# One recurrence step of a chunked delta rule with two head pairs on opposite quarters of the array

## The chip, the cores and the metric

The kernel runs on one core of one Trainium2 chip. The metric is the time of one execution in device microseconds. Engines: PE is TensorE, DVE is VectorE, ACT is ScalarE, POOL is GpSimd, SP is SyncE, which issues the DMAs.

## What is computed

One decoder layer on 512 tokens of width 1024: a combined projection, dilated attention, RWKV-7 time mixing, two branch gates, an output projection and a gated feed-forward network with a short convolution. Everything is float32; the large products are made of three products of rounded float32 halves (hi x hi, hi x lo, lo x hi), each with 512 moving columns. The part that the change touches is the recurrence of the time mixing, over 16 heads of 64 channels:

```python
def step(state, inp):
    r_t, w_t, k_t, v_t, aa_t, bb_t = inp
    sa = jnp.einsum('bhvk,bhk->bhv', state, aa_t)
    state = state * w_t[:, :, None, :] + sa[..., None] * bb_t[:, :, None, :] + v_t[..., None] * k_t[:, :, None, :]
    return state, jnp.einsum('bhvk,bhk->bhv', state, r_t)

_, y = lax.scan(step, state0, (tm(r_h), tm(w_h), tm(k_h), tm(v_h), tm(-kk), tm(kk * a_h)))
mean = jnp.mean(y, axis=-1, keepdims=True)
var = jnp.mean(jnp.square(y - mean), axis=-1, keepdims=True)
y = ((y - mean) * lax.rsqrt(var + GN_EPS)).reshape(b, s, c) * lnx_w + lnx_b
```

## The kernel before

**Groups, pairs, chunks.** The 512 tokens are cut into 8 chunks of 64 (`NCH`, `C`). The 16 heads make 8 pairs of 128 channels, two pairs make a group, and the four groups are worked through in turn. For a pair, `pair()` makes the projections k, r and v (24 products each), the decays, the tile `ar` (in each chunk 64 columns of a-rows and 64 of r-rows), the tile `bk` and the products of both, the gram tile `gt`, masked on DVE (`mask`, L1396). `inverse(g)` (L1429) then inverts the triangular blocks of a group: a long row of small DVE instructions, two batches of 32x32 products on PE (`pe`), and copies on DVE and ACT. `chain(g)` (L1565) runs the recurrence of the group's two pairs, chunk by chunk.

**One chunk of a chain**, in the order in which it must happen: `state` (L1610) adds the products of the state `mbd` with `ar` (two of 128 rows by 128 columns of the array) and of the values with `gt` (four of 64 by 64) in a PSUM tile `xy`. Half of its partitions, `X`, is the right side of the solve, the other half, `R`, the start of the chunk's output; which is which changes with the parity of the chunk, because a pair's tiles hold even and odd chunks with their halves swapped. `xs` (L1619) copies the half `X`, 64 partitions by 256 columns (two pairs side by side), to SBUF on ACT; `solve` (L1629) multiplies it with the inverse (four of 64 by 64); an ACT copy (L1658) brings the result, again 64 by 256, into the other half of the tile `uv`; `update` (L1633) makes the state's addition `w` from it (four of 128 by 64, which alternate between the two column halves), `carry` (L1638) scales and adds on DVE into `mbd`, with `mp` from POOL. Off this path `outs` (L1645) adds the last part of the output in `xy[R]`, and `out` (L1649) copies it into `yts`. Every second chunk `values` (L1584) centres the next two chunks' values and two ACT copies (`value`) put them into `uv`. After the chain `norm` scales `yts`, `turn` (L1710) transposes it, and `y` and `gated` (L1719, L1723) finish each pair on DVE. A float32 product is recorded as two MATMUL rows.

**What sets the order.** `Plan` (L47) simulates the engines with a cost in microseconds for each task and writes the instructions in the order in which its engines would take them. A chain's steps have priority 0 and go first; the 512-column products fill PE in between: while chains 0 to 2 run, the projections of the groups to come (k, r, v) and 16 branch gates (`pg` with 512 columns); while chain 3 runs, the attention's output projection (`pa`). A pair of group 2 can start only when chain 0 has given its buffers back, one of group 3 when chain 1 has, and a chain needs its group's inverse. After chain 3 `rwkv_out` and everything behind it run in the order of the code. The order is fixed when the kernel is built: on the chip every engine takes its own instructions strictly in that order and waits where data is late.

Of the kernel before, what the change touches and what calls it, by code (L numbers as in the profile page):

```python
# [18 lines left out]
P = 128  # L19
# [109 lines left out]
class Layer:  # L129
# [278 lines left out]
    def begin(self):  # L408
        self.rw_ctx = ExitStack()
        one = ("col wv v12 o1 row qk00 qk10 qk01 qk11 qk02 qk12 t kk2 fb fk ein cs bk rk km sh l2 l2l gp0 gp1 inv xs mp g2 "  # L410
               "sq yts").split()
        two = "raw w mm sp acc ht wvraw v0 attT sc sm pr pts pt po araw2 acc2 px xy k gg y ld psb".split()
        self.pl = Plan(**{x: 1 for x in one}, **{x: 2 for x in two}, uv=3, araw=10, ekraw=4)
# [809 lines left out]
    def pair(self, g, i):  # L1223
# [20 lines left out]
        def halves(t, x):  # L1244

            f = t.rearrange("p (t e) n -> p t (e n)", e=2)
# [75 lines left out]
        def a_row():  # L1322
            d["ar"] = gp.tile([P, NCH, P], F32, tag="ar", name=self.n("ar"), bufs=2)

            d["bkt"] = [gp.tile([P, 4, P], F32, tag="bkt", name=self.n("bkt")) for q in range(2)]
            nc.vector.scalar_tensor_tensor(halves(d["ar"], 1), c8(d["k"]), ch(self.kkn), pex(), op0=ALU.mult,
                                           op1=ALU.mult)
# [5 lines left out]
        ar = dve(0.75, a_row, [k, ex, gr["room"]])  # L1333
# [6 lines left out]
        def norm():  # L1340

            pn = d["pn"] = self.psx("pn")
            for t in range(4):
                self.mm(pn[:, 2 * t : 2 * t + 2], d["kk2"][:, t * P : (t + 1) * P], self.sel2, t == 0, t == 3)

        def norms():
            if i == 0:
                gr["sq"] = gp.tile([P, 16], F32, tag="sq", name=self.n("sq"), bufs=1)
            for x in range(2):
                nc.scalar.copy(gr["sq"][64 - 64 * x : 128 - 64 * x, 8 * i : 8 * i + 8], d["pn"][64 * x : 64 * x + 64, :8])  # L1350
# [33 lines left out]
        def gram(q):  # L1384
# [4 lines left out]
            for cc in range(4):  # L1389
                col = (cc % 2) * 2 + cc // 2  # L1390
# [174 lines left out]
    def chain(self, g):  # L1565
# [18 lines left out]
        def values(c):  # L1584
            for i in range(2):
                self.mm(d["u"][:, i * P : (i + 1) * P], prs[i]["v"][:, c * C : (c + 2) * C], self.cen, i == 0, i == 1)

        def value(c, x):
            uv = uvs[c + x] = cw.tile([P, 256], F32, tag="uv", name=self.n("uv"), bufs=3)
            nc.scalar.copy(uv[64 * x : 64 * x + 64, :], d["u"][64 * x : 64 * x + 64, :])  # L1590
# [5 lines left out]
        norms, all_ = [], []  # L1596

        def vals(c):
            t = pe(0.54, lambda: values(c), [start, last_uv])
            for x in range(2):  # L1600
                uvd[c + x] = sca(0.38, lambda x=x: value(c, x), [t], C_ + 0.01 * x, take=("uv",))
        vals(0)
        for c in range(NCH):
            e, q, cp = c % 2, c // 4, (c % 4) // 2
            r0, x0 = (0, 64) if e == 0 else (64, 0)
            R, X = slice(r0, r0 + 64), slice(x0, x0 + 64)
            gt = lambda i, h, rows, cols, e=e, q=q, cp=cp: prs[i]["gt"][rows, e, 4 * q + 2 * cp + h, cols]
# [11 lines left out]
            def xs(s=s, X=X):  # L1619
                s["xs"] = cw.tile([P, 256], F32, tag="xs", name=self.n("xs"), bufs=1)  # L1620
                nc.scalar.copy(s["xs"][X, :], s["xy"][X, :256])
# [23 lines left out]
            def outs(c=c, s=s, gt=gt, R=R):  # L1645
                for j, (i, h, cs) in enumerate(hs):
                    self.mm(s["xy"][R, cs], gt(i, h, slice(0, P), R), s["uv"][:, cs], c == 0 and j == 0, j == 3)

            def out(c=c, s=s, R=R):  # L1649
                if c % 2 == 0:  # L1650
                    yts[c // 2] = cw.tile([P, 256], F32, tag=f"yt{c // 2}", name=self.n("yt"), bufs=1)
                nc.scalar.copy(yts[c // 2][R, :], s["xy"][R, :256])

            st = pe(1.1 if c else 0.56, state, [uvd[c], start] + mb, take=("xy",), name=f"xy{g}.{c}")
            x = sca(0.38, xs, [st], take=("xs",))
            mpt = pl.add("POOL", 1.06, mp, mb, C_, take=("mp",)) if 0 < c < NCH - 1 else None
            so = pe(0.56, solve, [x, last_uv], give=("xs",), name="u")
            last_uv = sca(0.38, lambda s=s, X=X: nc.scalar.copy(s["uv"][X, :], d["u"][X, :]), [so])  # L1658
            prev = mb
            if c < NCH - 1:  # L1660
                up = pe(0.5, update, [last_uv], name="w")
                mb = [dve(0.36, lambda i=i, carry=carry: carry(i), [up, mpt], give=("mp",) if mpt and i else ())
# [3 lines left out]
            ou = pe(0.47, outs, [last_uv], C_ + 0.02, name="xr")  # L1666
            yt = sca(0.38, out, [ou], C_ + 0.05, take=("yts",) if c == 0 else (), give=("xy",))
            pl.join([ou] + ([up] if c < NCH - 1 else []), give=("uv",))
# [7 lines left out]
        fin = []  # L1676
        for i in range(2):
# [32 lines left out]
            def turn(i=i):  # L1710
                ys["p", i] = py = ps("t")
                for t in range(4):
                    self.tr(py[:, t * P : (t + 1) * P], yts[t][:, i * P : (i + 1) * P], t == 0, t == 3)

# [3 lines left out]

            def y(i=i, m=m):  # L1719
                nc.vector.scalar_tensor_tensor(ys[i], ys["p", i], self.col["lnx_w"][:, m : m + 1], ys[i],  # L1720
                                               op0=ALU.mult, op1=ALU.add)
# [10 lines left out]
            yl = pl.add("DMA", 0.8, y_load, [d["yt", 5], prs[i]["bvs"]], M_, take=("y",), lag=2.0)  # L1732
            tu = pe(0.95, turn, norms, min(S_, T_), take=("t",), name="ty")
            fin.append(tu)
            t = dve(0.75, y, [tu, yl], E_, give=("t",))
            t = dve(0.75, gated, [t, gt_], T_, give=("gg",))
# [10 lines left out]
    def norm(self, yts, t, deps, T_):  # L1747
# [3 lines left out]
        y4 = lambda: yts[t].rearrange("p (h e) -> p h e", e=64)  # L1751
# [386 lines left out]
```

## Time and profile before

| what | value |
|---|---|
| three runs | 1253.78, 1249.96, 1244.15 us; median 1249.96 |
| profiled execution, its own time | 1247.44 us |
| its span, first to last instruction | 1245.7 us |
| PE busy | 1197.4 us (96%) |
| DVE, ACT, POOL busy | 746.5, 545.4, 118.2 us |
| chain 0, first product to last | 441.7 to 493.0 us of the span |
| chain 3, first product to last | 714.9 to 766.8 us of the span |

In the timeline a row is a run of like instructions; the difference between the starts of two rows that follow each other on PE is what the first took of PE's time, since products overlap at their ends. A name such as `128*64` says which part of the array a product holds: 128 rows (the depth of the sum) by 64 columns (output partitions).

### The profile page before, as it was taken

What the parts mean: (1) busy time and instruction counts of PE and PEld (TensorE: products, weight loads), DVE (VectorE), ACT (ScalarE), POOL (GpSimd) and SP (SyncE); (2) the same over time, 40 slices, a digit from 0 to 9 for tenths busy, and PEclk for the clock granted to TensorE, in tenths of its full rate; (3) what the DMA queues carried; (4) which work ended last, traced back from release to release, by engine and by line L of the source; (5) the groups of instructions that cost most, each with busy time, mean ns of one, the idle gap of its engine ahead of it and who ended that gap; (6) DMA issues with size and microseconds to landing.
All of it is one profiled execution on the core that took longest, in us unless ns stands there. A gap on an engine that the chain in (4) does not pass through costs nothing.

```text
span 1245.7 us, 18047 instructions
## 1 busy us (share of the span) xinstructions
PE 1197.4 (96%) x7012; PEld 976.5 (78%) x7012; DVE 746.5 (60%) x1242; ACT 545.4 (44%) x981; POOL 118.2 (9%) x235
## 2 busy tenths in 40 slices
PE   4999999999999999999999799999999999999997
PEld 3788878888787877777787577788888888878886
DVE  6697862422678968536896844555556566552235
ACT  4484522523566373455445343334443434442133
POOL 4000000000001013030002222214100000000001
PEclk9899999999999999999999789999999999999999
DMA  9745871130333332322330424571133332323331
GB/s 316 242 143 163 274 235 49 46 85 1 92 99 88 97 89 77 110 60 82 92 105 26 146 79 132 174 219 34 56 97 96 90 102 85 102 87 116 102 119 68
DMA packets 168900, 139.39 MB, mean 112 GB/s; under 512 B 8849, under 2 KB 150251, under 8 KB 168815
## 3 DMA queue, kind: packets, MB, share of 16 engines
q1 hardware_dynamic: 168671, 137.98, 36.5%
q8 instruction: 55, 0.90, 0.3%
q14 instruction: 30, 0.25, 0.1%
q10 hardware_dynamic: 144, 0.26, 0.1%
HBM read 127.65 MB, written 10.56 MB: 111 GB/s over the span
## 4 chain that ended last, share of the span: by engine, by line
PE 82%; DVE 8%; DMA 5%; ACT 2%; issue 1%; SPq 0%; POOL 0%; POOLq 0%; DVEq 0%; ACTq 0%
PE u L148 23%; PE o L148 13%; PE v L148 7%; PE pg L148 7%; PE qk L148 6%; PE xy L148 4%; PE pr L148 3%; DMA araw<-in_w_ada_dram 3%; PE k L148 3%; PE pa L148 2%; PE r L148 2%; PE early L148 2%; PE po L148 2%; PE sc L148 1%; PE pt L151 1%
## 5 line engine op out<-in xcount | busy, mean ns | idle before, releaser
L194 DVE TENSOR_TENSOR wlo<-raw,whi 128x1024 fp32r<-128x1024 f32 x67 | 84.1, 1255 | 151.0 <-ACT whi L193 150.9
L148 PE MATMUL u<-h2lo,whi 128*128 128x512 f32 (+2 forms) x368 | 142.3, 387 | 0.0
L148 PE MATMUL u<-h2hi,whi 128*128 128x512 f32 (+2 forms) x368 | 142.3, 387 | 0.0
L148 PE MATMUL u<-h2hi,wlo 128*128 128x512 f32 (+2 forms) x368 | 142.2, 386 | 0.0
L1136 ACT CAST whi<-raw 128x1024 fp32r<-128x1024 f32 (+2 forms) x73 | 72.5, 993 | 130.2 <-PE qk L148 49.5
L193 ACT CAST whi<-raw 128x1024 fp32r<-128x1024 f32 x67 | 70.3, 1049 | 112.0 <-PE o L148 53.8
L1139 DVE TENSOR_TENSOR wlo<-raw,whi 128x1024 fp32r<-128x1024 f32 (+2 forms) x73 | 84.2, 1154 | 22.9 <-ACT whi L1136 22.7
L148 PEld LDWEIGHTS u<-h2hi,wlo 128*128 128x128 f32 x368 | 68.9, 187 | 15.7
L148 PEld LDWEIGHTS u<-h2lo,whi 128*128 128x128 f32 x368 | 68.9, 187 | 15.7 <-POOL h2lo L405 0.2
L148 PEld LDWEIGHTS u<-h2hi,whi 128*128 128x128 f32 x368 | 68.9, 187 | 15.5
L1983 DVE SCALAR_TENSOR_TENSOR u<-u,cols,u 128x511 f32<-128x511 f32 x88 | 65.6, 746 | 4.2 <-ACT u L1981 2.7
L148 PE MATMUL qk<-hhi,wlo 128*128 128x512 f32 x160 | 63.9, 400 | 0.0
L148 PE MATMUL qk<-hlo,whi 128*128 128x512 f32 x160 | 63.6, 397 | 0.0
L148 PE MATMUL qk<-hhi,whi 128*128 128x512 f32 x160 | 63.5, 397 | 0.0
L148 PE MATMUL o<-whi,fhi 128*128 128x512 f32 x144 | 56.1, 390 | 0.3 <-DVE u L1983 0.3
L148 PE MATMUL o<-wlo,fhi 128*128 128x512 f32 x144 | 56.0, 389 | 0.0
L148 PE MATMUL o<-whi,flo 128*128 128x512 f32 x144 | 56.0, 389 | 0.0
L148 PE MATMUL pg<-hhi,wlo 128*128 128x512 f32 x128 | 52.0, 406 | 0.0
L148 PE MATMUL pg<-hlo,whi 128*128 128x512 f32 x128 | 51.8, 405 | 0.0
L148 PE MATMUL pg<-hhi,whi 128*128 128x512 f32 x128 | 51.3, 401 | 0.0
L810 DVE CUSTOM_DVE_ANT_0 sm<-sc,m 128x256 f32<-128x256 f32 (+1 forms) x64 | 24.0, 405 | 37.6 <-PE sc L148 36.5
L347 DVE SCALAR_TENSOR_TENSOR acc<-araw,cols,acc 128x1024 f32<-128x1024 f32 x28 | 35.9, 1282 | 17.2 <-DMA araw<-in_w_ada_dram 17.1
(404 smaller groups left out, 2824.0 us busy)
## 6 DMA issues: line engine op xcount, KB each, us to landing
raw<-in_w_in_dram SPq DMA_DIRECT2D x62, 512.0 KB
raw<-in_w_up_dram SPq DMA_DIRECT2D x44, 512.0 KB
araw<-in_w_ada_dram SPq DMA_DIRECT2D x32, 512.0 KB
raw<-in_w_down_dram SPq DMA_DIRECT2D x22, 512.0 KB
araw<-in_w_ada_dram SPq DMA_DIRECT2D x32, 256.0 KB
wvraw<-in_w_in_dram SPq DMA_DIRECT2D x20, 256.0 KB
gate_d<-gs SPq DMA_DIRECT2D x16, 256.0 KB
gate<-gate_d SPq DMA_DIRECT2D x16, 256.0 KB
```

The lines of the kernel that those rows point to most:

```text
L148: return self.nc.tensor.matmul(out, lhsT, rhs, start=start, stop=stop)
L151: self.nc.tensor.matmul(out, in_, self.ident[: in_.shape[0], : in_.shape[0]], is_transpose=True, start=start, stop=stop,)
L193: self.nc.scalar.copy(hl[0], raw)
L194: (lo_eng or self.nc.vector).tensor_tensor(hl[1], raw, hl[0], op=ALU.subtract)
L347: nc.vector.scalar_tensor_tensor(d["acc"], raw, ck, d["acc"], op0=ALU.mult, op1=ALU.add)
L810: nc.vector.tensor_tensor_reduce(d["sm", h][:, :wd], d["sc"][h][:, :wd], m[:, 256 - wd : 256] if gi == 0 else m[:, :wd], 1.0, 3.0e38, op0= ...
L1136: nc.scalar.copy(d["w"][0], d["raw"])
L1139: nc.vector.tensor_tensor(d["w"][1], d["raw"], d["w"][0], op=ALU.subtract)
L1983: nc.vector.scalar_tensor_tensor(u[:, d:], pu[:, : S - d], ch(c), u[:, d:], op0=ALU.mult, op1=ALU.add)
```

## The change

A group's second pair is stored with its halves swapped (`x ^= i` in `halves`). Its gram tile, inverse and chunk halves swap with it, so that in every chunk the first pair's `R` and `X` are the second pair's `X` and `R`. Both pairs then use the same 128 columns of `xy`, on opposite partitions, and in `state`, `solve` and `outs` the products of the two pairs follow each other by turns (`ih`), on different rows and columns of the array. The output half leaves `state` for a task and a PSUM tile of its own, `state_out` and `xo`, so `state` has two products of 128 by 64 where it had two of 128 by 128, and `state_out` has two more. `xs` and `out` copy 128 partitions by 128 columns instead of 64 by 256. The copy after `solve` becomes two, one for each pair (64 by 128). `values` has four products of 128 by 64 with 128 columns each for two of 128 by 128. `uv` holds two chunks, `xy` and `xo` have one buffer each, where `xy` had two. At the end of a group each of two transposed tiles holds half of both pairs, so `y` is four DVE instructions on half tiles. For the second pair `ar` is written by two instructions. The planner's costs are changed to fit: `state` 1.1 to 0.6, `solve` 0.56 to 0.33, the copies 0.38 to 0.28 or 0.29, `outs` 0.47 to 0.35.

```diff
         def values(c):
-            for i in range(2):
-                self.mm(d["u"][:, i * P : (i + 1) * P], prs[i]["v"][:, c * C : (c + 2) * C], self.cen, i == 0, i == 1)
+            for n, i, x in ((0, 0, 0), (0, 1, 0), (1, 1, 1), (1, 0, 1)):
+                r = 64 * (i ^ x)
+                self.mm(d["u"][r : r + 64, n * P : n * P + P], prs[i]["v"][:, (c + x) * C : (c + x + 1) * C], self.cen,
+                        n == 0, n == 1)
...
-            def state(c=c, q=q, s=s, gt=gt, R=R, X=X):
-                xy = s["xy"] = ps("xy", bufs=2)
-                s["uv"] = uvs.pop(c)
-                if c:
-                    for i in range(2):
-                        self.mm(xy[:, i * P : (i + 1) * P], prs[i]["ar"][:, c, :], mbd(i), i == 0, False)
-                for j, (i, h, cs) in enumerate(hs):
-                    self.mm(xy[X, cs], gt(i, h, R, X), s["uv"][R, cs], c == 0 and j == 0, j == 3)
+            ih = [(i, h, slice(h * 64, h * 64 + 64), slice(i * P + h * 64, i * P + h * 64 + 64)) for h in range(2) for i in range(2)]
+
+            def state(c=c, s=s, gt=gt, R=R, X=X, ih=ih):
+                xy = s["xy"] = ps("xy")
+                s["uv"] = uvs[c - c % 2][:, c % 2]
+                for i in range(2 if c else 0):
+                    self.mm(xy[X[i], :P], prs[i]["ar"][:, c, X[i]], mbd(i), True, False)
+                for i, h, cs, ci in ih:
+                    self.mm(xy[X[i], cs], gt(i, h, R[i], X[i]), s["uv"][R[i], ci], c == 0 and h == 0, h == 1)
+
+            def state_out(c=c, s=s, R=R):
+
+                s["xo"] = ps("xo")
+                for i in range(2 if c else 0):
+                    self.mm(s["xo"][R[i], :P], prs[i]["ar"][:, c, R[i]], mbd(i), True, False)
...
-            def solve(s=s, gt=gt, X=X):
-                for j, (i, h, cs) in enumerate(hs):
-                    self.mm(d["u"][X, cs], gt(i, h, X, X), s["xs"][X, cs], j == 0, j == 3)
+            def solve(s=s, gt=gt, X=X, ih=ih):
+                for i, h, cs, _ in ih:
+                    self.mm(d["u"][X[i], cs], gt(i, h, X[i], X[i]), s["xs"][X[i], cs], h == 0, h == 1)
+
+            def solved(i, s=s, X=X):
+                nc.scalar.copy(s["uv"][X[i], i * P : i * P + P], d["u"][X[i], :P])
...
-            st = pe(1.1 if c else 0.56, state, [uvd[c], start] + mb, take=("xy",), name=f"xy{g}.{c}")
-            x = sca(0.38, xs, [st], take=("xs",))
+            st = pe(0.6 if c else 0.33, state, [uvd[c], start] + mb, take=("xy",), name=f"xy{g}.{c}")
+            so_ = pe(0.33 if c else 0.0, state_out, [st], C_ + 0.01, take=("xo",), name="xo")
+            x = sca(0.29, xs, [st], take=("xs",), give=("xy",))
...
-            so = pe(0.56, solve, [x, last_uv], give=("xs",), name="u")
-            last_uv = sca(0.38, lambda s=s, X=X: nc.scalar.copy(s["uv"][X, :], d["u"][X, :]), [so])
+            so = pe(0.33, solve, [x, last_uv], give=("xs",), name="u")
+            last_uv = sca(0.28, lambda solved=solved: solved(0), [so])
+            last_uv = sca(0.28, lambda solved=solved: solved(1), [last_uv])
```

On PE, in chain 3, one chunk from the state's products to the products behind the solve, before (`mbd` is the state, `xs` the copied right side, `pa` the 512-column products that fill PE, each row one product unless it says x4):

```order
L148 MATMUL xy_7136<-mbd_88,ar_5684 128x128
L148 MATMUL xy_7136<-mbd_89,ar_6137 128x128
L148 MATMUL xy_7136<-uv_7073,gt_5848 64x64 x4
L148 MATMUL pa_7095<-ahi,wlo_7028 128x512
L148 MATMUL pa_7146<-ahi,whi_7090 128x512
L148 MATMUL pa_7146<-alo,whi_7090 128x512
L148 MATMUL pa_7146<-ahi,wlo_7091 128x512
L148 MATMUL u_6815<-xs_7144,gt_5848 64x64 x4
```

And the same stretch of the changed kernel:

```order
L148 MATMUL xy_7284<-mbd_88,ar_5718 64x128
L148 MATMUL xy_7284<-mbd_89,ar_6205 64x128
L148 MATMUL xy_7284<-uv_7213,gt_5851 64x64 x4
L148 MATMUL xo_7291<-mbd_88,ar_5718 64x128
L148 MATMUL xo_7291<-mbd_89,ar_6205 64x128
L148 MATMUL pa_7241<-alo,whi_7173 128x512
L148 MATMUL pa_7241<-ahi,wlo_7174 128x512
L148 MATMUL u_6943<-xs_7294,gt_5851 64x64 x4
```

The output half (`xo`) stands behind the right side, and two filling products are left between it and the solve, where there were four. Between the solve and the update there are five where there were four.

On DVE, at the end of group 3's inverse (`tt` and `lt` are its tiles, `pe` the 32x32 products; `var` belongs to chain 2's norm, `alo` and `wlo` to the work that fills PE in chain 3), before:

```order
L1514 STREAM_TRANSPOSE tt_6435<-tt_6435 128x32x16
L1519 STREAM_TRANSPOSE lt_6408<-tt_6435 128x512
L1759 TENSOR_REDUCE var_6713<-sq_6687 128x4
L1560 COPY lt_6408<-pe_6718 32x512
L1808 TENSOR_TENSOR alo<-ld_6702,ahi 128x512
L1808 TENSOR_TENSOR alo<-ld_6704,ahi 128x512
L1562 COPY gt_5848<-pe_6718 32x16x32
```

And in the changed kernel, from the same transpose to the first of the two copies:

```order
L1521 STREAM_TRANSPOSE tt_6527<-tt_6527 128x32x16
L1765 SCALAR_TENSOR_TENSOR y_6683<-t_6824,cols,y_6683 128x4x64
L1765 SCALAR_TENSOR_TENSOR y_6696<-t_6824,cols,y_6696 128x4x64
L1526 STREAM_TRANSPOSE lt_6496<-tt_6527 128x512
L1844 TENSOR_TENSOR alo<-ld_6802,ahi 128x512
L1765 SCALAR_TENSOR_TENSOR y_6683<-t_6840,cols,y_6683 128x4x64
L1765 SCALAR_TENSOR_TENSOR y_6696<-t_6840,cols,y_6696 128x4x64
L1844 TENSOR_TENSOR alo<-ld_6804,ahi 128x512
L1139 TENSOR_TENSOR wlo_6833<-raw_6810,whi_6832 128x512
L1139 TENSOR_TENSOR wlo_6852<-raw_6816,whi_6851 128x512
L1567 COPY lt_6496<-pe_6856 32x512
```

Two of chain 2's four `y` instructions now stand ahead of the inverse's last transpose (L1519 before, L1526 now), and two `y`, two `alo` and two `wlo` ahead of the copy of its first products (L1560 before, L1567 now).

## Rows read from the trace of the kernel before

**Rows 1.** Page, part 1: busy time of each engine.

```profile
PE 1197.4 (96%) x7012; PEld 976.5 (78%) x7012; DVE 746.5 (60%) x1242; ACT 545.4 (44%) x981; POOL 118.2 (9%) x235
```

**Rows 2.** Windows: stretch, its length, busy of each engine, granted clock, DMA share, GB/s.

```profile
550.00:600.00 50.00, 49.94 (x320) 38.91 (x321) 29.76 (x45) 24.72 (x45) 6.64 (x14) 1.00 0.29 85
600.00:650.00 50.00, 49.20 (x361) 39.28 (x359) 46.57 (x85) 23.70 (x38) 1.01 (x4) 1.00 0.37 100
...
705.00:710.00 5.00, 1.92 (x64) 1.78 (x64) 3.06 (x5) 2.70 (x6) 1.82 (x3) 0.50 0.52 155
...
725.00:730.00 5.00, 5.00 (x33) 3.75 (x31) 1.89 (x5) 2.85 (x8) 0.00 (x0) 0.95 0.18 56
```

**Rows 3.** Timeline of PE in chain 3: start, duration, product, part of the array, count.

```profile
738.52 0.60 PE L148 MATMUL xy<-mbd,ar 128*128 128x128 f32 x4
739.05 0.68 PE L148 MATMUL xy<-uv,gt 64*64 64x64 f32 x8
739.66 0.50 PE L148 MATMUL pa<-ahi,wlo 128*128 128x512 f32 x1
...
740.79 0.67 PE L148 MATMUL u<-xs,gt 64*64 64x64 f32 x8
741.39 0.50 PE L148 MATMUL pa<-ahi,whi 128*128 128x512 f32 x1
...
742.52 0.45 PE L148 MATMUL u<-uv,bkt 128*64 128x64 f32 x8
742.90 0.71 PE L148 MATMUL u<-cen,v 128*128 128x128 f32 x4
743.54 0.68 PE L148 MATMUL xy<-uv,gt 128*64 128x64 f32 x8
744.15 0.50 PE L148 MATMUL pa<-alo,whi 128*128 128x512 f32 x1
744.49 0.40 PE L148 MATMUL pa<-ahi,wlo 128*128 128x512 f32 x1
744.72 0.61 PE L148 MATMUL xy<-mbd,ar 128*128 128x128 f32 x4
...
748.73 0.45 PE L148 MATMUL u<-uv,bkt 128*64 128x64 f32 x8
749.01 0.63 PE L148 MATMUL xy<-uv,gt 128*64 128x64 f32 x8
749.57 0.50 PE L148 MATMUL pa<-ahi,wlo 128*128 128x512 f32 x1
```

**Rows 4.** Timeline of PE: products that alternate between parts of the array, elsewhere.

```profile
508.15 1.20 PE L148 MATMUL pe<-lt,gt 32*32 32x32 f32 x64
509.29 0.50 PE L148 MATMUL pg<-hhi,wlo 128*128 128x512 f32 x1
...
663.54 1.16 PE L148 MATMUL pg<-ar,bk 64*128 64x128 f32 x16
664.63 0.45 PE L148 MATMUL u<-uv,bkt 128*64 128x64 f32 x8
```

**Rows 5.** Groups on ACT: copies out of PSUM, count, busy, mean ns, idle before.

```profile
L1621 ACT COPY xs<-xy 64x256 f32<-64x256 f32 x32 | 11.7, 367 | 28.9 <-PE xy L148 28.6
L845 ACT COPY o<-po 128x128 f32<-128x128 f32 x16 | 4.2, 266 | 15.0 <-PE po L148 15.0
```

**Rows 6.** Timeline of DVE: last masks and ends of the inverses of groups 2 and 3.

```profile
593.05 1.29 DVE L1397 TENSOR_TENSOR gt<-pg,mask 128x512 f32<-128x512 f32 x2 [0.36 <-PE pg L148]
...
644.88 0.71 DVE L1519 STREAM_TRANSPOSE lt<-tt 128x512 f32<-128x512 f32 x1
...
666.99 0.68 DVE L1397 TENSOR_TENSOR gt<-pg,mask 128x512 f32<-128x512 f32 x1
...
706.42 0.71 DVE L1519 STREAM_TRANSPOSE lt<-tt 128x512 f32<-128x512 f32 x1
...
714.54 0.27 DVE L1582 MEMSET u<- 128x256 f32 x1
```

More of the change, by code (lines that the diff above doesn't have):

```diff
@@ L409, in begin @@
         self.rw_ctx = ExitStack()
-        one = ("col wv v12 o1 row qk00 qk10 qk01 qk11 qk02 qk12 t kk2 fb fk ein cs bk rk km sh l2 l2l gp0 gp1 inv xs mp g2 "
+        one = ("col wv v12 o1 row qk00 qk10 qk01 qk11 qk02 qk12 t kk2 fb fk ein cs bk rk km sh l2 l2l gp0 gp1 inv xs mp g2 xo xy "
                "sq yts").split()
-        two = "raw w mm sp acc ht wvraw v0 attT sc sm pr pts pt po araw2 acc2 px xy k gg y ld psb".split()
-        self.pl = Plan(**{x: 1 for x in one}, **{x: 2 for x in two}, uv=3, araw=10, ekraw=4)
+        two = "raw w mm sp acc ht wvraw v0 attT sc sm pr pts pt po araw2 acc2 px k gg y ld psb".split()
+        self.pl = Plan(**{x: 1 for x in one}, **{x: 2 for x in two}, uv=2, araw=10, ekraw=4)
         self.bodies = 0
@@ L1244, in halves @@
         def halves(t, x):
+            x ^= i
             f = t.rearrange("p (t e) n -> p t (e n)", e=2)
@@ L1325, in a_row @@
             d["bkt"] = [gp.tile([P, 4, P], F32, tag="bkt", name=self.n("bkt")) for q in range(2)]
-            nc.vector.scalar_tensor_tensor(halves(d["ar"], 1), c8(d["k"]), ch(self.kkn), pex(), op0=ALU.mult,
-                                           op1=ALU.mult)
+            for e in (range(2) if i else (slice(0, 2),)):
+                nc.vector.scalar_tensor_tensor(halves(d["ar"], 1)[:, :, e], c8(d["k"])[:, :, e], ch(self.kkn), pex()[:, :, e],
+                                               op0=ALU.mult, op1=ALU.mult)
         def k_row():
@@ L1595, in chain @@
         mb, uvd, last_uv = [], {}, start
-        norms, all_ = [], []
+        norms, all_, used = [], [], []
         def vals(c):
             t = pe(0.54, lambda: values(c), [start, last_uv])
-            for x in range(2):
-                uvd[c + x] = sca(0.38, lambda x=x: value(c, x), [t], C_ + 0.01 * x, take=("uv",))
+            t = sca(0.38, lambda: value(c, 0), [t], C_, take=("uv",))
+            uvd[c] = uvd[c + 1] = sca(0.38, lambda: value(c, 1), [t], C_)
         vals(0)
@@ L1661, in chain @@
                 up = pe(0.5, update, [last_uv], name="w")
-                mb = [dve(0.36, lambda i=i, carry=carry: carry(i), [up, mpt], give=("mp",) if mpt and i else ())
+                mb = [dve(0.36, lambda i=i, carry=carry: carry(i), [up, mpt, so_], give=("mp",) if mpt and i else ())
                       for i in range(2)]
@@ L1665, in chain @@
                 vals(c + 1)
-            ou = pe(0.47, outs, [last_uv], C_ + 0.02, name="xr")
-            yt = sca(0.38, out, [ou], C_ + 0.05, take=("yts",) if c == 0 else (), give=("xy",))
-            pl.join([ou] + ([up] if c < NCH - 1 else []), give=("uv",))
+            ou = pe(0.35, outs, [last_uv, so_], C_ + 0.02, name="xr")
+            yt = sca(0.29, out, [ou], C_ + 0.05, take=("yts",) if c == 0 else (), give=("xo",))
+            used.extend([ou] + ([up] if c < NCH - 1 else []))
+            if e:
+                pl.join(used, give=("uv",))
+                used = []
             d["yt", c] = yt
@@ L1675, in chain @@
         g2, gg, ys = {}, {}, {}
-        fin = []
+        fin, after = [], []
         for i in range(2):
@@ L1708, in gate_out @@
                 nc.scalar.copy(gg[i], gg["p", i])
[L1710 to L1713, printed above, removed]
             def y_load(i=i):
@@ L1732, in chain, with turn, y @@
             yl = pl.add("DMA", 0.8, y_load, [d["yt", 5], prs[i]["bvs"]], M_, take=("y",), lag=2.0)
+            after.append((yl, gt_, gated, m))
+        ts = [[], []]
+        for x in range(2):
+            def turn(x=x):
+                ys["p", x] = py = ps("t")
+                for t in range(4):
+                    self.tr(py[:, t * P : (t + 1) * P], yts[t][:, x, :], t == 0, t == 3)
+            def y(i, x=x):
+                b = ys[i].rearrange("p (t e j) -> p t e j", e=2, j=C)[:, :, x, :]
+                c = ys["p", x].rearrange("p (t e j) -> p t e j", e=2, j=C)[:, :, i ^ x, :]
+                m = prs[i]["m"]
+                nc.vector.scalar_tensor_tensor(b, c, self.col["lnx_w"][:, m : m + 1], b, op0=ALU.mult, op1=ALU.add)
             tu = pe(0.95, turn, norms, min(S_, T_), take=("t",), name="ty")
             fin.append(tu)
-            t = dve(0.75, y, [tu, yl], E_, give=("t",))
-            t = dve(0.75, gated, [t, gt_], T_, give=("gg",))
+            for i in range(2):
+                ts[i].append(dve(0.45, lambda i=i, y=y: y(i), [tu, after[i][0]], E_, ))
+            pl.join([ts[i][-1] for i in range(2)], give=("t",))
+        for i, (yl, gt_, gated, m) in enumerate(after):
+            t = dve(0.75, gated, [*ts[i], gt_], T_, give=("gg",))
             if g < 2:
```

44 lines of the change are left out of this document (23 added, 21 removed).

## Prediction

> **What bounds the kernel now.** I read the page first, for the engine that is always busy: PE, 96% of the span [rows 1]. Then the windows, for whether that holds while the chains run. From 550 to 600 us PE is busy 49.94 of 50 us and DVE 29.76: PE sets the pace. From 600 to 650 DVE is busy 46.57: it makes group 3's inputs and group 2's inverse, and PE, still full, works off gates that nothing waits for yet. From 705 to 710 PE is busy 1.92 of 5 us at a granted clock of 0.50 (1.2 GHz), because its filling work is used up and chain 3 waits for DVE's inverse; at 725 to 730 the clock is back at 0.95 of 2.4 GHz [rows 2]. Then the timeline of DVE, for the places where the lead passes from PE to DVE: the last mask of group 2 ends at 594.3, its inverse at 645.6; the last mask of group 3 ends at 667.7, its inverse at 707.1, and chain 3's first PSUM tile is cleared at 714.5 [rows 6]. So there are three kinds of time: PE-bound from chain 0's start (441.7) to about 594, DVE-bound to about 714, PE-bound again through chain 3 and to the end. A microsecond of PE saved in the second stretch is worth little.
>
> Last the timeline of PE, for what a chunk costs. From start to start [rows 3]: the two state products 0.53 (738.52 to 739.05), the gt products behind them 0.61, the solve 0.60, the update 0.28 (748.73 to 749.01), the outs 0.56. That is 2.58 us of small products in a chunk; the rest are fillings of 0.23 each (744.49 to 744.72; the first behind a change of the form takes 0.34). Every second chunk has also the values, 0.64 (742.90 to 743.54), and then the update before them takes 0.38 and the outs behind them 0.61.
>
> **What the change does to a chunk's PE time.** Three rows show the price of products that alternate. The update, whose blocks alternate between column halves, takes 0.28 for 8 rows where the outs, same block and same width but always one column half, take 0.56 [rows 3]. The grams alternate between row halves: 16 rows of 128 columns take 1.09, 0.068 each, where a state product's row of 128 columns over the whole array takes 0.53 / 4 = 0.13 [rows 3, 4]. The 32x32 products change rows and columns at once, in one PSUM tile, and take 1.14 / 64 = 0.018 a row [rows 4], half of what the outs' 0.07 for twice the width would give. So I take half price for all pairs by turns: state 4 rows at 0.068 = 0.27; gt 0.28; state_out 0.27 and 0.1 for one more change of form; solve 0.28; update 0.28 as before; outs 0.28. Sum 1.76 for 2.58, so -0.82. Values: 8 rows at 0.068 = 0.54 and, between products of the same form, without the two changes: update and values together 0.82 for 1.02, outs 0.28 for 0.61 where 0.56 was counted: about -0.25 in every second chunk, -0.12 on the mean. The first chunk of a chain has no state products, which leaves it nearly the same gain (0.61 + 0.60 + 0.56 become 0.84). I take **-0.9 us a chunk**, 32 chunks, 29 us of PE in all. From both sides: if nothing overlaps, the gt, solve and outs keep their price, and state, state_out and values double, +0.8 a chunk; if the 64x64 pairs overlap better than the outs' half, -1.1. The nearest rows are the update and the 32x32 ones, so -0.9.
>
> The Trainium skill has a rule against this, in "TensorEngine Tiling (Array Packing)", section Restrictions and Gotchas: different row tiles cannot use the same PSUM bank at the same time. Here the pairs' 64x64 products are different row tiles and write one tile; the 32x32 rows do so too and come out at half price, so the trace speaks against it for this form. By that rule gt and solve would stay at 0.61 and 0.60; it is the first rival below. The same page, section Tiling Modes, says that a change of the tiling mode drains the engine; the trace's update takes 0.38 before the values' 128x128 form and 0.28 before its own, 0.1 us a change, which is in the sum.
>
> **Latency of a chunk.** PE gains this time only if the next step is ready when PE comes to it. Copies: 128 columns take 0.27 (the nearest ACT row, 128x128 out of PSUM), 256 columns 0.37 [rows 5]. So `xs` gains 0.1 and the copy behind the solve, now two, takes 0.54 for 0.37. In the new order state_out and two fillings (0.27 + 0.1 + 0.57) cover the 0.27 copy; five fillings (1.27) cover the two copies; outs and four fillings cover the carry. `xo` has one buffer, so the next state_out also waits for the copy `out`; four fillings and the next state's products, 1.5 us, stand between. No step should wait, and nothing is lost here; if the double copy did wait, it would be 0.2 a chunk.
>
> **What of it reaches the end**, in order:
> 1. Chain 0's start to group 2's last mask (441.7 to 594.3), PE-bound: 16 chunks at 0.9 = -14.4. In the new order 353 products of 512 columns stand in this stretch for 344, as more gates come early: 9 at 0.23 = +2.1. **-12.3.**
> 2. Group 2's inverse (594.3 to 645.6), DVE-bound: DVE has one `km` and one `wlo` less there. A 128x512 instruction is 0.65 (half of the masks' 1.29 [rows 6]), a `wlo` twice as wide; up to -1.9, with waits on ACT between them **-1.5**.
> 3. Chain 2's start to group 3's last mask: the grams stand behind its first chunks, which are shorter, and behind 9 fillings for 12: **-2.5**. The rest of chain 2's gain lies beside DVE's inverse and only lengthens PE's pause before chain 3.
> 4. Group 3's inverse and its tail (667.7 to 714.5), DVE-bound and longer: as chain 2 is quicker, two more carries, two half-width `y`, a `km`, a `var` and two small ones fall between mask and last transpose, about 3 us by the 0.65 above (estimates, narrower ones at 0.35 to 0.4). In the tail two `y`, two `alo`, two `wlo` stand before the copy of the inverse's products, 3.4 us where 2.0 us pass now; they also wait for loads that start when chain 2 ends: +2. **+5**, between -3 (less waiting for chain 2's carries, which now come earlier) and +9.
> 5. Chain 3 to the output projection, PE-bound, with 176 products of 512 columns before and after: 8 chunks at 0.9 = -7.2, and four transposes stand ahead of the chain now, -0.5. **-7.7.**
>
> The sum is -19.0. Behind it nothing changes. The granted clock falls in the pause before chain 3 in both kernels; the pause is some 8 us longer, but the work at the low clock is the same first chunk of chain 3, so I take 0, between -3 and +3. The added DVE instructions for the second pair's `ar` and the 0.25 us they cost a group lie before the masks in PE-bound time. Against the profiled execution's 1247.44 the sum gives 1228.4. The median of the runs shown is 2.5 above it, inside their spread of 10; I forecast **1229 us**, own range 1222 to 1236. A difference of 1% is about what a measurement of this kernel can tell from no change.
>
> **Rivals.**
> - *Row tiles in one bank take turns.* gt and solve keep 0.61 and 0.60; a chunk gains 0.9 - 0.33 - 0.32 = 0.25. For it speaks only that the grams, which overlap, write two tiles; against it the 32x32 rows [rows 4]. Steps 1, 3 and 5 become 16 x 0.25 - 2.1 = -1.9, -0.7 and -2.5, steps 2 and 4 stay: -1.6, **1246**. Chance 0.13.
> - *All of it reaches the end.* DVE's waits for the carries shrink with the chain, step 4 becomes -3: -27, **1220**. For it: DVE now waits for chain 2 inside the inverse; against: the new instructions in its way. Chance 0.14.
> - *DVE or the weights hold group 2's and 3's projections back.* Then steps 1 to 3 vanish into waits and chain 3 alone gains, -7.7, step 4 costs nothing on top of it since its instructions have slack: **1240**. Against: DVE 29.76 of 50 between 550 and 600 [rows 2]. Chance 0.09.
> - *Slower: alternation over rows and columns is not free for the float32 passes.* Place: every small product of all 32 chunks. If each row keeps its full price, a chunk costs +0.8 (above): 16 x 0.8 + 2.1 = +14.9, step 3 about +2, steps 2 and 4 as they are, step 5 +6: +26, **1274**. It decides from the point where a chunk's small products take more than the 2.58 of now. Against it: all three rows of alternating products. Chance 0.05.
>
> My forecast has 0.59. **Range** 1219 to 1243: it leaves out the slower case and most of the first rival. Faster by over 1% (under 1237.5): the forecast but for its upper edge, and the second: 0.72. Within 1%: most of the first and third: 0.22. Slower by over 1%: 0.06.
>
> **What would show it.** In the timeline of PE: gt, solve and outs at 0.28 to 0.31 for 8 rows, state and state_out at 0.27 to 0.37; chunks of chain 3 at 4.8 us where 5.65 and 6.2 stand now. On DVE: group 2's last mask near 582, its inverse near 632, group 3's last mask near 651, chain 3's clear near 700. Chain 3's first product to the first output product shorter by 7 to 8 us. Wrong would be: the 64x64 rows at 0.6 (first rival), rows of PE waiting for the double copy, masks of group 2 after 590 (third), or DVE waiting for `y`, `alo` or `wlo` before the inverse's copy for more than 4 us.

## The result, and the profile after

The changed kernel takes **1231.91 us** (median of 4 runs, 1229.57 to 1233.42) where the kernel before takes 1249.1 (4 runs): ratio 0.9862, 95% interval 0.9835 to 0.9889, so 1.4% faster. The forecast was 1229 with an own range of 1222 to 1236 and a wider one of 1219 to 1243; both hold. A second measurement gave 1230.25 (5 runs) and 0.9856 (0.9836 to 0.9876). The profiled execution has 1231.16 us and a span of 1229.4, against 1247.44 and 1245.7: 16.3 less.

The engines' busy times on the page of the changed kernel, beside [rows 1]:

```profile
PE 1179.8 (96%) x7188; PEld 946.3 (77%) x7188; DVE 746.0 (61%) x1254; ACT 542.6 (44%) x1009; POOL 120.3 (10%) x235
```

PE has 176 rows more and 17.6 us of busy time less. DVE and ACT have hardly changed.

The timeline of PE in chain 3 of the changed kernel, one chunk and the start of the next, and the values of a chunk that has them (to be read as [rows 3], by the difference between starts):

```profile
732.91 0.44 PE L148 MATMUL xy<-mbd,ar 128*64 128x128 f32 x4
733.28 0.45 PE L148 MATMUL xy<-uv,gt 64*64 64x64 f32 x8
733.66 0.44 PE L148 MATMUL xo<-mbd,ar 128*64 128x128 f32 x4
734.03 0.50 PE L148 MATMUL pa<-ahi,wlo 128*128 128x512 f32 x1
734.37 0.40 PE L148 MATMUL pa<-ahi,whi 128*128 128x512 f32 x1
734.70 0.45 PE L148 MATMUL u<-xs,gt 64*64 64x64 f32 x8
735.07 0.50 PE L148 MATMUL pa<-alo,whi 128*128 128x512 f32 x1
...
736.11 0.40 PE L148 MATMUL pa<-ahi,wlo 128*128 128x512 f32 x1
736.43 0.45 PE L148 MATMUL u<-uv,bkt 128*64 128x64 f32 x8
736.72 0.40 PE L148 MATMUL xo<-uv,gt 128*64 128x64 f32 x8
737.05 0.50 PE L148 MATMUL pa<-ahi,whi 128*128 128x512 f32 x1
...
737.85 0.39 PE L148 MATMUL pa<-ahi,whi 128*128 128x512 f32 x1
738.17 0.44 PE L148 MATMUL xy<-mbd,ar 128*64 128x128 f32 x4
...
741.97 0.61 PE L148 MATMUL u<-cen,v 128*64 128x128 f32 x8
742.40 0.40 PE L148 MATMUL xo<-uv,gt 128*64 128x64 f32 x8
```

State 0.37, gt 0.38, state_out 0.37, solve 0.37, update 0.29, outs 0.33, values 0.43. Before they were 0.53, 0.61, none, 0.60, 0.28, 0.56 and 0.64. The fillings (the 512-column products) say something too: 734.37 to 734.70 and 736.11 to 736.43 are 0.33 and 0.32 for a product of 0.23, so 0.1 goes to the change to another part of the array, and 737.85 to 738.17 is one more such change, which the old chunk, whose state products used the whole array as the fillings do, did not have (744.49 to 744.72 in [rows 3]). This chunk, from 732.91 to 738.17, is 5.26 us with 11 fillings; without them 5.26 - 11 x 0.233 = 2.70, and a chunk with values has 3.13. In the kernel before it was 3.09 and 3.87. So a chunk has become 0.40 or 0.74 shorter, 0.57 on the mean.

The timeline of DVE of the changed kernel, where it answers to [rows 6]: the last masks of groups 2 and 3, the last transposes of their inverses, and the clear of chain 3's PSUM tile:

```profile
586.69 1.28 DVE L1404 TENSOR_TENSOR gt<-pg,mask 128x512 f32<-128x512 f32 x2
...
634.47 0.71 DVE L1526 STREAM_TRANSPOSE lt<-tt 128x512 f32<-128x512 f32 x1
...
651.35 1.29 DVE L1404 TENSOR_TENSOR gt<-pg,mask 128x512 f32<-128x512 f32 x2 [1.75 <-PE pg L148]
...
695.18 0.69 DVE L1526 STREAM_TRANSPOSE lt<-tt 128x512 f32<-128x512 f32 x1
...
705.49 0.27 DVE L1589 MEMSET u<- 128x256 f32 x1
```

With the ends of these rows the 16.3 us fall to the five steps of the prediction so (chain 0 starts at the same time to 0.2 us, and from the first output product, at 791.11 and now at 774.83, to the end both spans have 454.6):

| step | before | after | difference | predicted |
|---|---|---|---|---|
| 1, to group 2's last mask | 594.3 | 588.0 | -6.4 | -12.3 |
| 2, group 2's inverse | 51.2 | 47.2 | -4.0 | -1.5 |
| 3, to group 3's last mask | 22.1 | 17.5 | -4.6 | -2.5 |
| 4, to chain 3's clear | 46.9 | 52.9 | +6.0 | +5 |
| 5, to the first output product | 76.6 | 69.3 | -7.2 | -7.7 |

### The profile page after: what moved, and what is told of

Read it like the earlier page. It is cut to its first block, busy times and chain, and to the rows that moved or that the text cites. A ratio compares the mean times of both kernels' runs of the same rounds, so it can differ in the third digit from the quotient of the medians.

```text
span 1229.4 us, 18443 instructions
## 1 busy us (share of the span) xinstructions
PE 1179.8 (96%) x7188; PEld 946.3 (77%) x7188; DVE 746.0 (61%) x1254; ACT 542.6 (44%) x1009; POOL 120.3 (10%) x235
## 4 chain that ended last, share of the span: by engine, by line
PE 82%; DVE 9%; DMA 4%; ACT 2%; issue 1%; SPq 0%; POOL 0%; POOLq 0%; DVEq 0%; ACTq 0%
PE u L148 22%; PE o L148 13%; PE v L148 7%; PE pg L148 7%; PE qk L148 6%; PE pr L148 3%; PE r L148 3%; PE k L148 3%; PE pa L148 3%; DMA araw<-in_w_ada_dram 2%; PE early L148 2%; PE po L148 2%; PE xy L148 2%; PE pt L151 1%; PE xo L148 1%
```

## The experiments

The executions differ before chain 0 is reached, where the programs are nearly the same: its clear (of its PSUM tile, as chain 3's above) falls between 439.6 and 445.3 us. From 180 to 200 us, where PE waits for some 2 to 3 us, the granted clock was 1.00 in some and 0.83 to 0.91 in others, that is, at the lower of its two levels for part of the stretch. So the profiles are compared from chain 0's clear on, and the medians are read beside them. Each ratio is to executions of the kernel before that were taken beside that run. The profile of the changed kernel's second measurement has 264.0, 332.6 and 787.2 in the last three columns, so a difference of about 1 us there says nothing by itself. All times in us:

| run | median | ratio to before (95%) | chain 0's clear | from there to chain 3's clear | to the first output product | to the span's end |
|---|---|---|---|---|---|---|
| before | 1249.1 | | 441.4 | 273.2 | 349.8 | 804.3 |
| changed | 1231.9 | 0.9862 (0.9835 to 0.9889) | 441.2 | 264.3 | 333.7 | 788.2 |
| no turns | 1234.5 | 0.9889 (0.9858 to 0.9919) | 442.8 | 265.7 | 335.0 | 789.7 |
| turns, same quarter | 1247.5 | 1.0000 (0.9986 to 1.0013) | 440.4 | 273.2 | 349.9 | 804.6 |
| costs alone | 1253.6 | 1.0035 (1.0010 to 1.0060) | 442.3 | 277.4 | 350.5 | 809.6 |
| old costs | 1233.9 | 0.9876 (0.9855 to 0.9896) | 445.3 | 258.3 | 330.0 | 787.0 |
| gt first | 1231.3 | 0.9862 (0.9844 to 0.9880) | 442.3 | 262.6 | 331.1 | 785.7 |
| transposes late | 1232.1 | 0.9864 (0.9845 to 0.9883) | 445.1 | 261.0 | 331.4 | 785.9 |
| both, gt first in odd chunks | 1225.9 | 0.9817 (0.9802 to 0.9831) | 439.6 | 259.3 | 328.3 | 782.9 |
| the same with old costs | 1230.4 | 0.9852 (0.9833 to 0.9871) | 443.7 | 256.7 | 328.3 | 786.2 |

**Are the turns what overlaps?** First the turns were taken away and all else kept:

```diff
-            ih = [(i, h, slice(h * 64, h * 64 + 64), slice(i * P + h * 64, i * P + h * 64 + 64)) for h in range(2) for i in range(2)]
+            ih = [(i, h, slice(h * 64, h * 64 + 64), slice(i * P + h * 64, i * P + h * 64 + 64)) for i in range(2) for h in range(2)]
```

> The changed kernel, but in the gt products of state, in solve and in outs the products of one pair follow each other (both of the first pair, then both of the second) instead of by turns. Stored halves, copies, order of everything else stay. Theory (neighbours on different rows and columns overlap, and that is the whole gain): the 8 rows of gt go from 0.38 back to about 0.61, solve from 0.38 to 0.60, outs from 0.33 to 0.56, +0.7 us a chunk; 16 chunks up to group 2's last mask +11, 8 in chain 3 +5.5, some of chain 2's beside DVE: about 1249 us, no different from the kernel before. Rival (the gain comes from the smaller copies and the split of the state's products): the rows stay below 0.45 and the time stays at 1232.

PE's timeline in chain 3 of this run:

```profile
736.04 0.45 PE L148 MATMUL xy<-uv,gt 64*64 64x64 f32 x8
736.43 0.44 PE L148 MATMUL xo<-mbd,ar 128*64 128x128 f32 x4
...
737.46 0.46 PE L148 MATMUL u<-xs,gt 64*64 64x64 f32 x8
737.84 0.50 PE L148 MATMUL pa<-alo,whi 128*128 128x512 f32 x1
...
739.49 0.45 PE L148 MATMUL xo<-uv,gt 128*64 128x64 f32 x8
739.87 0.50 PE L148 MATMUL pa<-ahi,whi 128*128 128x512 f32 x1
```

Gt 0.39, solve 0.38, outs 0.38: only outs lost 0.05. The theory as it stood has fallen. What the rival forecast came, but its reason does not fit the rows: the state's products, split, take more than before (0.37 and 0.37 for 0.53), and smaller copies do not shorten a solve whose data is there. PE waited for `xs` ahead of the solve for 1.2 us in the whole kernel before, and not at all in the changed one. What is left is the second quarter. The counterpart is the kernel before with turns on its one quarter (in state's gt part, solve and outs):

```diff
-                for j, (i, h, cs) in enumerate(hs):
+                for j, (i, h, cs) in enumerate(hs[::2] + hs[1::2]):
...
```

> The kernel before, with the products of the two pairs by turns in the gt part of state, in solve and in outs, but on one and the same quarter of the array, as there. The run without turns kept 0.38 for gt and solve, so the first theory (neighbours must differ) has fallen. New theory (what counts is that two quarters hold the work at all; the array takes the second pair's products while the first's still run, in whatever order they stand): turns on one quarter change nothing, gt 0.61, solve 0.60, outs 0.56, 1249 us. Rival (turns between two columns of the output tile are what is quick): gt and solve below 0.45, 1238 us or less.

PE's timeline there:

```profile
740.01 0.68 PE L148 MATMUL u<-xs,gt 64*64 64x64 f32 x8
740.61 0.50 PE L148 MATMUL pa<-ahi,whi 128*128 128x512 f32 x1
```

The solve stays at 0.60, and the time is that of the kernel before. So turns without a second quarter give nothing, and a second quarter without turns gives nearly all. The single records of a solve show how. Behind a first gap of 0.1 us its rows start one by one, 58 ns apart, in the kernel before; in the changed kernel they start in twos, 6 to 7 ns between the two and 58 from one two to the next; without turns in twos as well, 13 to 14 ns between them. The records do not name the quarter; the reading is that each quarter takes a row every 58 ns, and that the second pair's rows do not wait behind the first pair's. The two pairs differ in rows and in columns of the array; whether one of these would do for 64x64 products was not run. The Trainium skill says under "TensorEngine Tiling (Array Packing)", Tiling Modes, that different tiles can load weights and multiply in parallel; these runs agree, at 0.38 for 0.60. The Trainium skill's rule on the same page, under Restrictions and Gotchas, that row tiles cannot use the same PSUM bank at the same time, does not hold for this form: the pairs' twos write one PSUM tile, on opposite partitions.

**Is it the order that the planner makes?** The change has shorter products and lower costs; each was run without the other. The costs alone, in the kernel before:

```diff
-            st = pe(1.1 if c else 0.56, state, [uvd[c], start] + mb, take=("xy",), name=f"xy{g}.{c}")
-            x = sca(0.38, xs, [st], take=("xs",))
+            st = pe(0.93 if c else 0.33, state, [uvd[c], start] + mb, take=("xy",), name=f"xy{g}.{c}")
+            x = sca(0.29, xs, [st], take=("xs",))
...
-            so = pe(0.56, solve, [x, last_uv], give=("xs",), name="u")
+            so = pe(0.33, solve, [x, last_uv], give=("xs",), name="u")
...
```

> The kernel before, planned with the changed kernel's costs (state 0.93, solve 0.33, copies 0.29 and 0.56, outs 0.35), its products as they were: the order without the shorter products. 350 products of 512 columns stand from chain 0's first product to group 2's last mask for 344. Theory (the gain is the products'): no gain, +1.4 at that mask, 1249 to 1251 us. Rival (a good part of the gain is the order that the lower costs make): 1243 or less.

It is slower by 0.35% (interval 0.10 to 0.60%): the order alone gains nothing. Group 2's last mask comes 0.6 us later than before, counted from chain 0's clear; most of the loss lies behind the first output product (459.1 us to the end for 454.6). The products alone, under the old costs:

```diff
-            st = pe(0.6 if c else 0.33, state, [uvd[c], start] + mb, take=("xy",), name=f"xy{g}.{c}")
-            so_ = pe(0.33 if c else 0.0, state_out, [st], C_ + 0.01, take=("xo",), name="xo")
-            x = sca(0.29, xs, [st], take=("xs",), give=("xy",))
+            st = pe(1.1 if c else 0.56, state, [uvd[c], start] + mb, take=("xy",), name=f"xy{g}.{c}")
+            so_ = pe(0.0, state_out, [st], C_ + 0.01, take=("xo",), name="xo")
+            x = sca(0.38, xs, [st], take=("xs",), give=("xy",))
...
```

> The changed kernel, planned with the costs of the kernel before (state 1.1 with nothing for state_out, solve 0.56, copies 0.38, outs 0.47). The order then has 143 products of 512 columns between the first products of chains 0 and 1 for 182, and 200 from there to group 2's last gram for 171. Theory (chain 1 starts when DVE has finished group 1's inverse, whatever PE saved in chain 0): chain 1 starts at 513 to 514 us as now, PE waits before it, and 29 more fillings of 0.23 make group 2's last mask 5 to 7 us later: about 1237 us. Rival (PE's sum decides): 10 fillings fewer, -2.3, 1229.5.

Neither came. Group 2's last mask is 0.9 us later, chain 1 starts 6.4 us earlier (65.8 us after chain 0's clear for 72.2). DVE's inverse of group 1 was not fixed in time, as I had taken it: with 39 fillings less beside chain 0, four `y`, two `gated` and a `wlo` fell behind the inverse on DVE, whose stretch from the last mask to the last transpose went from 48.2 to 41.4 us (busy 38.8 to 34.5). The 29 fillings that came after chain 1's start then took the 6.4 us back. Chain 3 starts 6.0 us earlier than in the changed kernel, is 2.4 longer, and 2.4 more are lost behind the first output product: to the span's end the run is 1.2 us under the changed kernel, about as far as two profiles of that one lie apart, and the medians cannot tell them apart. The gain is the products'.

**What does a change of the array's form cost?** The gt products were put ahead of the state's, so that both products with the state stand together, with one change fewer:

```diff
-                for i in range(2 if c else 0):
-                    self.mm(xy[X[i], :P], prs[i]["ar"][:, c, X[i]], mbd(i), True, False)
                 for i, h, cs, ci in ih:
-                    self.mm(xy[X[i], cs], gt(i, h, R[i], X[i]), s["uv"][R[i], ci], c == 0 and h == 0, h == 1)
+                    self.mm(xy[X[i], cs], gt(i, h, R[i], X[i]), s["uv"][R[i], ci], h == 0, c == 0 and h == 1)
+                for i in range(2 if c else 0):
+                    self.mm(xy[X[i], :P], prs[i]["ar"][:, c, X[i]], mbd(i), False, True)
```

> The changed kernel, with the gt products of state ahead of the state's own two, so that these and state_out, all of 128x64, stand together: one change of the form of the array fewer in 28 chunks, the same products otherwise. Theory (each change of form costs 0.1 us, which the sum of the prediction forgot): a chunk without its fillings takes 2.59 us without values and 3.03 with, for 2.69 and 3.13; 14 chunks before group 2's last mask -1.4, 7 in chain 3 -0.7: 1230 us. Rival (the time between rows is the products' own): 2.69 and 3.13 stay, 1232.

PE's timeline there, the state's products of an odd chunk, and gt and state at the start of an even one:

```profile
737.20 0.44 PE L148 MATMUL xy<-mbd,ar 128*64 128x128 f32 x4
737.47 0.39 PE L148 MATMUL xo<-mbd,ar 128*64 128x128 f32 x4
737.79 0.50 PE L148 MATMUL pa<-alo,whi 128*128 128x512 f32 x1
...
742.36 0.79 PE L148 MATMUL xy<-uv,gt 64*64 64x64 f32 x8
743.08 0.44 PE L148 MATMUL xy<-mbd,ar 128*64 128x128 f32 x4
```

State takes 0.27, as the prediction had it, and state_out 0.32 (0.37 there, with a change of form). From one state's start to the next it is 2.55 us without fillings where there is no gt of new values; here the theory holds, with 0.15 for a change less. But an even chunk's gt now takes 0.72: it stands ahead of the state's products and waits for the copy of the new values, which ACT makes here:

```profile
741.89 0.76 ACT L1602 COPY uv<-u 64x256 f32<-64x256 f32 x2 [2.41 <-DVE mbd L1664]
```

That copy waits for the carry on DVE, as the state's products do. The wait takes back in one chunk what the other gains (3.32 for 3.13). From chain 0's clear the run is 2.5 us under the changed kernel; its median is the same within the interval.

**What holds chain 3 back?** Chain 2's transposes were made to wait, in the plan, for the inverse's second batch of 32x32 products:

```diff
         p2 = pl.add("PE", 1.25, second_pe, ec, 0.5, name="pe")
+        if g == 3:
+            for tu in self.turns:
+                p2.users.append(tu)
+                tu.left += 1
...
             fin.append(tu)
+            self.turns = fin
```

> The changed kernel, but chain 2's transposes, and with them its four y instructions, wait in the plan for the second batch of 32x32 products of group 3's inverse. Theory (the products of the inverse wait for a PSUM tile that y gives back, and DVE's copies stand behind y, alo and wlo): from the start of the inverse's last DVE transpose to chain 3's first product 8.4 us as in the kernel before, for 10.6 now, -2.2; the transposes stand in chain 3 in exchange, up to +1: about 1230.5 us. Rival (alo and wlo, or the copies on ACT, hold it all the same): 10.6 stays, 1232 to 1233.

PE's timeline in the changed kernel, from the inverse's products to chain 3's first:

```profile
697.55 1.92 PE L148 MATMUL pe<-lt,gt 32*32 32x32 f32 x64 [1.06 <-DVE y L1765]
700.87 1.91 PE L148 MATMUL pe<-tt,lt 32*32 32x32 f32 x64 [1.40 <-DVE lt L1567]
705.82 1.12 PE L148 MATMUL u<-cen,v 128*64 128x128 f32 x8 [3.03 <-DVE u L1589]
```

And in this run:

```profile
699.34 1.92 PE L148 MATMUL pe<-lt,gt 32*32 32x32 f32 x64 [6.50 <-DVE lt L1526]
...
706.08 1.09 PE L151 MATMUL t<-ident,yt 128*128 128x128 f32 x4 [1.49 <-ACT gt L1573]
707.10 1.12 PE L148 MATMUL u<-cen,v 128*64 128x128 f32 x8
```

In the changed kernel the products of the inverse (`pe`) start 1.7 us after the transpose that they read (695.87), released by `y`, because `y` holds the PSUM tile that they need. In this run they follow it at once (699.29 to 699.34). From the start of that transpose to chain 3's first product it is 8.5 us for 10.6, as the theory had it, and chain 3's clear comes 3.3 us earlier after chain 0's. Not all of this is the tile: the wait for it was 1.6, from the first batch to the second it is 3.3 us in both runs, 1.2 come behind the second batch, where `gated` and what follows from `y` no longer stand, and 0.5 inside the inverse, where two `y` are gone. The transposes in chain 3 take 1 us back: 2.3 are left at the first output product (1.2 against the changed kernel's second profile). The medians agree within their intervals: this profile's first 440 us were 3.9 longer, with the clock at 0.83 from 180 to 200 us.

**A version that beats both.** The transposes late, and gt first only in odd chunks, whose values are old:

```diff
+                if e:
+                    for i, h, cs, ci in ih:
+                        self.mm(xy[X[i], cs], gt(i, h, R[i], X[i]), s["uv"][R[i], ci], h == 0, False)
                 for i in range(2 if c else 0):
-                    self.mm(xy[X[i], :P], prs[i]["ar"][:, c, X[i]], mbd(i), True, False)
+                    self.mm(xy[X[i], :P], prs[i]["ar"][:, c, X[i]], mbd(i), not e, e)
...
```

> The changed kernel, with the gt products ahead of the state's in odd chunks alone (in even ones they would wait for the copy of new values, 0.35 us, as the run with gt first shows), and with chain 2's transposes behind group 3's inverse. Theory (a change of form costs 0.1 us, and the tail of the inverse 3 us): from chain 0's first clear to the first output product 330.3 us for 333.7, odd chunks at 2.55 without their fillings, even ones at 3.13. Rival (the waits only move): 333 or more.

328.3 us to the first output product, 2 better than the theory. The theory named the chunks wrongly: the odd ones are those that make values, and went from 3.13 to 2.98, the even ones stayed at 2.69. The median is 1225.85. The same with the planner's old costs for chains 0 to 2:

> The run before this one, and the costs of the kernel before for chains 0 to 2. With them chain 1 started 6.4 us earlier, since 39 products less were put beside chain 0, and lost it again before group 2's last mask; chain 3 started 6.0 us earlier, and was 2.4 us longer with its old costs. Theory (what an order gains at chain 3's start adds to the others): clear to first output product about 328 us. Rival (the pause of PE before chain 3 is set by DVE whatever stands before): 330 as in the run before this.

The order gains nothing, as the rival said, but not for its reason: chain 3's clear does come 2.6 us earlier, and the first output product at the same 328.3. Behind it 3.4 us are lost again, and the median is 1230.4. All three runs with the other kernel's costs lose 2.4 to 4.5 us behind the first output product; in the first 30 us there PE does 103 to 113 rows where it does 122 in the changed kernel. The cause stays open. The better of the two was run once more, beside the changed kernel, on another chip:

> The changed kernel once more, beside the best variant on the same chip: ratio to the kernel before 0.984 to 0.989, about 1231 us.

> The run with gt first in odd chunks and chain 2's transposes late, once more. Theory (5.4 us less from chain 0's first clear to the first output product, as its profile showed): 4 to 6 us under the changed kernel on the same chip, ratio 0.980 to 0.983. Rival (part of its 1225.9 was only a clock that fell less before chain 0, where the programs are the same): 2 to 3 us under it, 0.984.

1230.25 (0.9856, 0.9836 to 0.9876) and **1225.17** (0.9815, 0.9795 to 0.9835): 5.1 us under the changed kernel.

## Why the prediction was right, and where it was not

**The mechanism** was read rightly from the update's and the 32x32 rows: products on two quarters overlap, and the first rival ("row tiles in one bank take turns") and the fourth ("slower") fell with that. "By turns" was read into it too much; the two runs above show that the quarters do it.

**-0.9 us a chunk was too much: 0.57 came.** The step that failed is the table of prices, "gt 0.28, solve 0.28, state 0.27". The 0.61 and 0.60 from which it started hold a change of form, the new prices left it out, though the same paragraph put 0.1 on state_out for it. The single records show it: eight rows of 58 ns are 0.47 of the old solve's 0.60, four twos are 0.23 of the new one's 0.37, and about 0.14 is left in both. Measured: state +0.10, gt +0.10, solve +0.09, outs +0.05, and 0.09 more in the filling ahead of the state, whose form is no longer that of the fillings; together 0.43, which is the whole gap of a chunk without values (0.82 predicted, 0.40 measured). Values were better than the estimate, 0.43 for 0.54.

**Step 1** (-12.3, measured -6.4) follows: 16 x 0.57 = -9.1, and the 9 fillings more, +2.1, make -7.0.

**Steps 2 and 3** (-4.0 together, measured -8.6) made up for most of it. The windows of both kernels, group 2's inverse, the stretch to group 3's last mask, group 3's inverse and its tail, with the columns of [rows 2]; before:

```profile
594.34:645.59 51.25, 50.45 (x250) 40.29 (x248) 45.80 (x85) 23.14 (x36) 1.20 (x4) 1.00 0.33 93
645.59:667.67 22.08, 21.88 (x286) 17.26 (x285) 15.87 (x27) 12.48 (x27) 1.88 (x5) 1.00 0.21 60
667.67:707.13 39.46, 33.36 (x268) 25.59 (x266) 31.01 (x73) 16.34 (x38) 12.44 (x22) 0.89 0.35 113
707.13:714.54 7.41, 4.46 (x131) 4.22 (x132) 3.68 (x7) 5.09 (x9) 1.82 (x3) 0.50 0.17 46
```

And after:

```profile
587.97:635.18 47.21, 46.85 (x237) 37.71 (x235) 43.74 (x83) 21.58 (x33) 3.11 (x4) 1.00 0.34 95
635.18:652.64 17.46, 17.40 (x264) 13.33 (x265) 13.95 (x25) 11.16 (x26) 1.53 (x4) 1.00 0.21 60
652.64:695.87 43.23, 35.17 (x339) 23.55 (x338) 33.79 (x82) 19.07 (x49) 14.82 (x25) 0.87 0.35 111
695.87:705.49 9.62, 4.45 (x131) 3.81 (x130) 7.34 (x13) 5.29 (x10) 0.00 (x0) 0.50 0.58 147
```

DVE's busy time (the third figure with a count) falls by 2.1 in the first row, for the `km` and the `wlo` that the prediction counted, and its idle time by 2.0 (5.45 to 3.47). In the second row it is 1.9 and 2.7: two carries and a `km` that stood ahead of the last mask now stand behind it. Idle time of DVE inside the inverse was not in the sum. So the total came near the forecast partly by luck: step 1 fell short by 5.9 us, and steps 2 and 3 gave 4.6 more than the sum had.

**Step 4** (+5, measured +6.0): the number came, the tail by another cause. In the third row DVE is busy 2.8 longer, for the carries, the `y`, the `alo` and the `km` that were counted from the order. In the fourth the tail is 2.2 longer, but not by the `y`, `alo` and `wlo` ahead of the copy of the inverse's products: from the first batch of these products to the second it is 3.32 us in both kernels. PE's rows before:

```profile
707.19 1.92 PE L148 MATMUL pe<-lt,gt 32*32 32x32 f32 x64 [2.92 <-DVE lt L1519]
710.51 1.92 PE L148 MATMUL pe<-tt,lt 32*32 32x32 f32 x64 [1.41 <-ACT lt L1560]
```

The first batch followed the transpose's end (707.13) by 0.1 us; now it follows (695.87) by 1.7, for the PSUM tile that `y` gives back. That is 1.6 of the 2.2. The other 0.6 lies behind the second batch (4.62 us to the clear for 4.03).

**Step 5** (-7.7, measured -7.2) is right by two errors. Six chunks with states are 3.4 us shorter and the last one some 0.4, not 7.2. The rest, 3.4, lies ahead of the second chunk, where the prediction had put no clock gain. The timeline of PE at the end of that time, before:

```profile
725.06 0.61 PE L148 MATMUL t<-sg,g2h 96*128 96x512 f32 x1
725.49 0.42 PE L148 MATMUL pa<-alo,whi 128*128 128x512 f32 x1
725.74 0.61 PE L148 MATMUL xy<-mbd,ar 128*128 128x128 f32 x4
```

And after:

```profile
710.94 0.63 PE L148 MATMUL pa<-alo,whi 128*128 128x512 f32 x1
711.37 0.56 PE L148 MATMUL pa<-ahi,wlo 128*128 128x512 f32 x1
...
712.57 0.40 PE L148 MATMUL t<-sg0h,g2h 128*128 128x512 f32 x1
712.81 0.40 PE L148 MATMUL t<-sg0l,g2h 128*128 128x512 f32 x1
```

A filling takes 0.43 at the lower level of the clock (1.2 GHz) and 0.23 at the upper one. Before, PE goes on at the lower level for 10.5 us of chain 3, with pauses for `xs`; in the changed kernel, which fills from the start, for some 6 (4.2 in its second profile). In 10.2 us up to the second chunk it does 21 fillings where it did 9 in 10.9. So "the work at the low clock is the same first chunk" was wrong. Not all of the 3.4 is the clock: four transposes (716.23 to 717.28, 1.05 us, for which the prediction took 0.5) and 0.8 of waits stood there before and are gone, and the first chunk's own products are shorter. The shares were not measured apart.

**Latency**: the copies came out as priced (`xs` takes 264 ns in the mean), and no step waits for the double one. The group on ACT after, beside [rows 5]:

```profile
L1654 ACT COPY uv<-u 64x128 f32<-64x128 f32 x64 | 16.7, 260 | 23.8 <-PE u L148 22.1 <-DVE tt L1514 1.1
```

PE's idle time ahead of update and outs, put down to the copies into `uv`, is 1.4 us over the whole kernel, against 1.3 before.

The second rival (all of it reaches the end) failed at step 4, the third (DVE holds groups 2 and 3 back) by group 2's last mask, which did come earlier.

## What to carry to other kernels

Put independent small products on different quarters of the array: here 8 rows of 64x64 cost 0.38 us for 0.60, whatever their order. Then count how often the stream changes the part of the array that it uses, each time about 0.1 us, and put products of one form side by side, unless that moves one ahead of data that it must wait for. Where the saving lies beside another engine's long chain, look at that engine's order for what now comes earlier: here 3.3 us before chain 3 were lost to `y` that had become ready too soon and what follows from it, half of it in a wait for the PSUM tile that `y` held.

## What was not expected of the hardware

That the order of the products does not matter for the overlap (0.38 with turns and without, rows of both pairs starting 7 or 14 ns apart). And the clock in chain 3: PE was back at the upper level 5.9 and 4.2 us after the chain's first product in two profiles of the changed kernel, where fillings follow at once, and 10.5 us after it in the kernel before, where PE paused for `xs`.
